# Two layers of a hybrid diffusion trunk: the second layer's modulation as elementwise products, the first step of the delta rule's inverse without matmuls, and another place for a buffer

## The chip, the cores and the metric

The kernel runs on one core of one Trainium2 chip. The metric is device time in microseconds of one execution. PE is the tensor engine, DVE the vector engine, ACT the scalar engine, POOL GpSimd, SP the sync engine, whose queue issues DMAs as POOL's does.

## What is computed

The program is one inference step of a trunk of two layers (DEPTH = 2) over 512 latent tokens and 128 context tokens, with 1024 channels. Each layer has a mixer (three parallel branches) and a feed-forward. What the change touches, cut from the reference:

```
mod = jax.nn.silu(cond) @ P['ada_w'][l] + P['ada_b'][l]          # 1024 x 6144, for two conditions
sh1, sc1, g1, sh2, sc2, g2 = jnp.split(mod[:, None, :], 6, axis=-1)
h = _rms(x, P['norm1_w'][l]) * (1 + sc1) + sh1
...                                                              # delta rule, HGRN2, attention
m = jnp.where(strict, jnp.einsum('nbhid,nbhjd->nbhij', kb, k) * decay, 0.0)
t_inv = lax.linalg.triangular_solve(eye + m, ...)                # inverse of eye + m, unit lower triangular
u = t_inv @ (v * beta[..., None]); w = t_inv @ (kb * jnp.exp(gc)[..., None])
...
x = x + g1 * (merged @ P['w_out'][l])
h = _rms(x, P['norm2_w'][l]) * (1 + sc2) + sh2
u = _dwconv(h @ P['w_up'][l], P['conv_ffn'][l]); a, u = jnp.split(u, 2, axis=-1)
x = x + g2 * ((jax.nn.silu(a) * u) @ P['w_down'][l])
```

## The kernel before

All 640 tokens are kept as columns; 128 channels are one tile in 128 partitions. Every large product is split into a high and a low half of each factor (hh and hl, or fh and fl, for activations, whi and wlo for weights): `k_steps` (line 907) issues six products for a block of 128 channels, 128x256 and 128x384 for each of three pairs, and `mtile` (line 914) eight such blocks for one output tile. A half tile of weights (4 blocks, 256 KB) is loaded on SP's queue into one of four raw buffers (wraw, line 839), copied to whi on ACT and subtracted to wlo on DVE (`w_tick`, line 878); the next load into a raw buffer waits for its wlo.

The order of the instructions on each engine is fixed when the program is built: `drive` (line 509) goes through the main stream (the large products) and side streams (the delta rule's two, HGRN2, attention, norm, the modulation), and takes a side stream's next piece when its due time, kept by cost formulas, is not ahead of PE's clock by more than a margin. Each engine then runs its own list in order.

The modulation of a layer is computed by a stream `ada` (line 693). For each chunk of 256 columns it loads four pieces of 128x2x256 (one chunk is 1 MB), issues eight products of cT, the condition as weights (32 columns), into 32 rows each, adds the result to `arows` on DVE (or copies it on ACT), and after `group` chunks turns `arows` into columns by two small products with c_sum. The first layer's chunks run ahead of and in the first mixer. The second layer's 24 chunks run in the first layer's feed-forward (line 2062), with two sets of raw buffers, in groups of four and with loads on POOL's queue. They must be done before the last group of the feed-forward goes down (line 2103).

The delta rule (`delta`, line 1219) handles five blocks in each layer: four heads' latent tokens and the context tokens. For a block of 4 x 128 tokens it inverts a triangular matrix by doubling: XC and XTC (the inverse of each 32x32 diagonal block and its transpose) start as beta on the diagonal (line 1303), and five steps (line 1306) merge blocks of 1, 2, 4, 8 and 16. A step is 16 products of 32x32 (`ath` by one half of XC), a masked product into `phc` on DVE, 16 products of 32x32 with the half of XTC, a 32x32-wise transpose on DVE and two subtractions. Two more merges, of 32 and 64, follow.

In the feed-forward (`ffn`, line 2045) the residual x is loaded back from DRAM by eight DMAs on POOL's queue, 320 KB each (line 2048), since its memory held the mixer's tiles. Then come the output projection with the update of x (`x_update`, line 2040, on DVE), norm, and three groups of up tiles (44 in all, with the depthwise conv on DVE) and down tiles (24). `open_f` (line 2024) allocates x first and fh after wx.

Of the kernel before, what the change touches and what calls it, by code (L numbers as in the profile page):

```python
# [7 lines left out]
F32 = mybir.dt.float32  # L8
F32R = mybir.dt.float32r
# [3 lines left out]
ALU = mybir.AluOpType  # L13
# [4 lines left out]
KD = 8  # L18
# [3 lines left out]
T = TS + TP  # L22
# [38 lines left out]
def shape_constants():  # L61
    c = np.zeros((128, N_CST), np.float32)
    p = np.arange(128)
    s, t = p[:, None], p[None, :]

    def put(i, a):
        c[:, i * 128:i * 128 + a.shape[1]] = a

    put(C_I, s == t)
    put(C_ONE, np.ones((128, 128)))  # L70
    put(C_UI, s <= t)
    put(C_LI, s >= t)
    put(C_US, s < t)
    put(C_LS, s > t)
    t32 = np.arange(32)[None, :]
    put(C_CP, np.concatenate([s % 32 == t32] + [(s % 32 // (2 << i) == t32 // (2 << i)) & (s % 32 >> i != t32 >> i)
                                                for i in range(5)], 1))
    misc = np.zeros((128, 128), np.float32)
    misc[:64, 2] = 1.0
    misc[64:, 3] = 1.0  # L80
    for g in range(4):
        for j in range(16):
            misc[32 * g + j, 8 + j] = 1.0
    for j in range(4):
        for e in range(2):
            misc[32 * j + e, 24 + 2 * j + e] = 1.0
    put(C_MISC, misc)
    nf = 16
    inv = (np.float32(10000.0) ** (-np.arange(nf, dtype=np.float32) / np.float32(nf))).astype(np.float32)
    pos = np.arange(TS)  # L90
    row, col = (pos // 64).astype(np.float32), (pos % 64).astype(np.float32)
    ang = np.where((p % 64 < 32)[:, None], row[None, :], col[None, :]).astype(np.float32) * inv[p % 16][:, None]
    put(C_COS, np.cos(ang.astype(np.float32)))
    put(C_SIN, np.sin(ang.astype(np.float32)) * np.where(p % 32 < 16, -1.0, 1.0).astype(np.float32)[:, None])
    return c
# [138 lines left out]
class Trunk:  # L234
# [325 lines left out]
    def setup(self):  # L560
# [14 lines left out]
        self.c_blk, self.c_pick = C(C_MISC)[:, 2:34], C(C_MISC)[:, 24:32]  # L575
        self.c_sum = C(C_MISC)[:, 8:24]
        self.hh = self.hp.tile([128, KD, T], F32R, name="hh")
        self.hl = self.hp.tile([128, KD, T], F32R, name="hl")
# [113 lines left out]

    def ada(self, l, chunks, raws, arows, gap=0.0, group=2, start=None):


        issued = 0
        at = []
# [20 lines left out]
        for n, j in enumerate(chunks):  # L718
# [22 lines left out]
            for q, j in enumerate(chunks[n - group + 1:n + 1]):  # L741
# [7 lines left out]
                self.post(("mod", l, j))  # L749
        self.post(("ada", l, chunks[-1]))  # L750

    def ada_tiles(self, pool, sets):
# [466 lines left out]
    def delta(self, l, w, batches):  # L1219
        sc, nc = dict(self.sc), self.nc  # L1220
        for name in ("ssk", "nk", "rk", "b0", "cq", "ss"):
            sc[name] = self.sc[name][:, w]
# [7 lines left out]
        for b in batches:  # L1230
# [30 lines left out]
            b0 = sc["b0"]  # L1261
            self.mul(b0, beta, bc(ssk, 1, 2))
            yield None
            pv, pq = self.psd(), self.psd()
# [30 lines left out]
            self.mul(att.ap, pqk, ph.ap)  # L1295

            small, phc = X.ap[:, 0, 0:128], ph.ap[:, 0:128]
            x64 = X.ap[:, 1, 0:256].rearrange("p (c x) -> p c x", c=4)
            self.zero(XT.ap)
            self.zero(x64)  # L1300
            XC, XTC = (xs.ap[:, o:o + 256].rearrange("p (d n) -> p d n", d=2) for o in (0, 256))
            c32 = XC.rearrange("p d (c x) -> p d c x", c=4)
            self.mul(c32, bc(bc(self.C(C_CP)[:, 0:32], 1, 4), 1, 2), bc(b0, 3, 32))
            self.cp(XTC, XC)
            yield None
            for i in range(5):
                m = 1 << i
# [516 lines left out]
    def mixer(self, l, x):  # L1824
# [13 lines left out]
        for name, shape in (("ab", [2, 2, 5, 4]), ("beta", [2, 5, 4]), ("g", [2, 5, 4]), ("gl", [2, 5, 4]), ("t0", [2, 5, 4]), ("t1", [2, 5, 4]),  # L1838
                            ("t2", [2, 5, 4]), ("ex", [3, 2, 5, 4]), ("neg", [2, 5, 4]), ("ssk", [2, 4]), ("nk", [2, 4]), ("rk", [2, 4]),
                            ("b0", [2, 2, 4]), ("cq", [2, 4]), ("ss", [2, 3, 4]), ("ssb", [3, 4]), ("ck", [3, 10]),  # L1840
                            ("s8", [3, 5, 8]),
# [171 lines left out]
        if l == 0:  # L2013
            self.spawn("ada", self.ada(0, range(8, 24), *self.ada_tiles(op, 1), 10000.0, 4))
        yield from gate_out(self.oa, "ga", self.col["norm_a"] + l)
# [8 lines left out]
    def open_f(self, l, first=False):  # L2024
        self.x_pool = ExitStack()
        fp = self.fp = self.x_pool.enter_context(self.tc.tile_pool(name=f"ffn{l}", bufs=1))
        x = fp.tile([128, KD, T], F32, name="x")
        self.N = [fp.tile([128, T], F32, name=f"N{j}") for j in range(3)]
# [5 lines left out]
        for S in self.S2[2:]:  # L2034
            self.zero_pads(S)
        self.fh = fp.tile([128, 8, T], F32R, name="fh")
        self.fl = fp.tile([128, 8, T], F32R, name="fl")
# [7 lines left out]
    def ffn(self, l, x):  # L2045
# [15 lines left out]
        if l + 1 < L:  # L2061
            self.spawn("ada", self.ada(l + 1, range(24), *self.ada_tiles(self.fp, 2), 12000.0, 4))
        n = 0
# [88 lines left out]
    def program(self):  # L2152
# [11 lines left out]
        self.spawn("ada", self.ada(0, (4, 0, 5, 1, 6, 2, 7, 3), *self.ada_tiles(init, 6), start=self.w_first))  # L2164
        self.step(self.sides[-1])
# [73 lines left out]
```

## Time and profile before

| | |
|---|---|
| time, median of 3 runs | 2730.98 us (2727.82 to 2731.32) |
| the profiled execution: its time, its span | 2731.32 us, 2729.5 us |
| PE busy | 2683.1 us (98%) |
| DVE busy | 1684.0 us (62%) |
| ACT busy | 1135.0 us (42%) |
| POOL busy | 216.1 us (8%) |
| DMA | 243.62 MB, 89 GB/s in the mean |
| large products of the mixers and feed-forwards | line 320, `mm` |
| small products of the side streams | lines 320 and 325, `sd` |

A product of two f32 tiles is two instructions on PE, so a group of eight shows as x16. The engine's name PEld stands for the loading of the stationary operand. The program's stages by time: the start to some 45 us, the first mixer to some 840, the first feed-forward to some 1385, the second mixer to some 2195, the second feed-forward to the end.

### The profile page before, as it was taken

What the parts mean: (1) busy time and instruction counts of PE and PEld (TensorE: products, weight loads), DVE (VectorE), ACT (ScalarE), POOL (GpSimd) and SP (SyncE); (2) the same over time, 40 slices, a digit from 0 to 9 for tenths busy, and PEclk for the clock granted to TensorE, in tenths of its full rate; (3) what the DMA queues carried; (4) which work ended last, traced back from release to release, by engine and by line L of the source; (5) the groups of instructions that cost most, each with busy time, mean ns of one, the idle gap of its engine ahead of it and who ended that gap; (6) DMA issues with size and microseconds to landing.
All of it is one profiled execution on the core that took longest, in us unless ns stands there. A gap on an engine that the chain in (4) does not pass through costs nothing.

```text
span 2729.5 us, 60705 instructions
## 1 busy us (share of the span) xinstructions
PE 2683.1 (98%) x25046; PEld 2558.5 (94%) x25046; DVE 1684.0 (62%) x4039; ACT 1135.0 (42%) x2619; POOL 216.1 (8%) x352
## 2 busy tenths in 40 slices
PE   8999999999999999999999999999999999999999
PEld 6999989989999999999999889899999999999999
DVE  6787865656545763554667887667566357545464
ACT  5555455534323431322345455545444244323232
POOL 1100101221001021120001001000000000000000
PEclk9999999999999999999999999999999999999999
DMA  8212223534225144443233112122222341222222
GB/s 265 71 39 53 67 57 96 158 114 126 59 76 161 58 144 132 147 143 101 80 92 83 47 45 67 49 74 73 57 61 55 82 124 56 78 73 75 77 76 80
DMA packets 356036, 243.62 MB, mean 89 GB/s; under 512 B 18069, under 2 KB 339137, under 8 KB 355632
## 3 DMA queue, kind: packets, MB, share of 16 engines
q1 hardware_dynamic: 334896, 175.94, 23.2%
q0 software_dynamic: 20432, 63.28, 7.1%
q8 instruction: 197, 3.23, 0.5%
q14 instruction: 79, 0.65, 0.1%
q10 hardware_dynamic: 432, 0.52, 0.1%
HBM read 225.79 MB, written 13.89 MB: 88 GB/s over the span
## 4 chain that ended last, share of the span: by engine, by line
PE 89%; DVE 6%; ACT 2%; issue 1%; DMA 1%; SPq 0%; ACTq 0%; DVEq 0%
PE mm L320 73%; PE sd L320 13%; PE sd L325 2%; DVE sl L355 1%; ACT sl L345 1%; DVE ex L355 1%; DMA wraw<-in_w_up_dram 1%; ACT ex L345 1%; DMA ar<-in_ada_w_dram 1%; DVE wlo L355 0%; SPq L430 0%; DVE N L368 0%; DVE Cv L368 0%; DVE x L368 0%; DVE ex L368 0%
## 5 line engine op out<-in xcount | busy, mean ns | idle before, releaser
L320 PE MATMUL mm<-hh,whi 128*128 128x256 f32 (+2 forms) x3696 | 873.8, 320 | 7.0 <-DVE x L368 6.0
L320 PE MATMUL mm<-hl,whi 128*128 128x256 f32 (+2 forms) x3696 | 841.6, 311 | 1.2 <-DVE hl L368 1.2
L320 PE MATMUL mm<-hh,wlo 128*128 128x256 f32 (+1 forms) x3632 | 835.8, 309 | 0.0
L320 PEld LDWEIGHTS mm<-hh,whi 128*128 128x128 f32 (+1 forms) x3696 | 644.3, 187 | 36.3 <-issue 25.1
L320 PEld LDWEIGHTS mm<-hl,whi 128*128 128x128 f32 (+1 forms) x3696 | 664.8, 187 | 4.0 <-DVE hl L368 1.8
L320 PEld LDWEIGHTS mm<-hh,wlo 128*128 128x128 f32 x3632 | 662.8, 188 | 0.0
L355 DVE TENSOR_TENSOR wlo<-wraw,whi 128x512 fp32r<-128x512 f32 x598 | 402.8, 680 | 369.6 <-ACT whi L345 368.6
L345 ACT ACTIVATE whi<-wraw 128x512 fp32r<-128x512 f32 x602 | 368.0, 618 | 282.4 <-PE mm L320 243.2
L368 DVE SCALAR_TENSOR_TENSOR Cv<-S,V,Cv 128x642 f32<-128x642 f32 x240 | 210.3, 883 | 2.2
L345 ACT ACTIVATE sl<-sd 128x512 f32<-128x512 f32 (+5 forms) x232 | 97.1, 429 | 195.3 <-PE sd L320 109.5
L345 ACT ACTIVATE sl<-sl 128x512 f32<-128x512 f32 (+6 forms) x224 | 119.4, 543 | 137.9 <-DVE sl L355 91.3
L320 PE MATMUL mm<-fh,whi 128*128 128x256 f32 (+1 forms) x704 | 166.7, 311 | 0.0
L320 PE MATMUL mm<-fl,whi 128*128 128x256 f32 (+1 forms) x704 | 164.7, 308 | 0.0
L320 PE MATMUL mm<-fh,wlo 128*128 128x256 f32 (+1 forms) x704 | 164.7, 308 | 0.0
L320 PE MATMUL sd<-sl,sl 128*32 128x32 f32 (+4 forms) x3384 | 156.8, 229 | 5.1 <-DVE sl L355 4.2
L430 POOL DMA_DIRECT2D ar<-in_ada_w_dram x160 | 113.3, 712 | 535.1 <-PE sd L320 528.5
L355 DVE TENSOR_TENSOR sl<-sl,sl 128x512 f32<-128x512 f32 (+2 forms) x212 | 148.9, 740 | 10.6 <-ACT sl L345 9.4
L320 PEld LDWEIGHTS sd<-sl,sl 128*32 128x32 f32 (+3 forms) x3384 | 124.8, 128 | 29.5 <-issue 12.6
L345 ACT ACTIVATE S<-mm 128x512 f32<-128x512 f32 x204 | 77.9, 435 | 160.9 <-PE mm L320 160.8
L368 DVE SCALAR_TENSOR_TENSOR x<-mm,mod,x 128x256 f32<-128x256 f32 (+1 forms) x192 | 74.6, 434 | 105.0 <-PE mm L320 100.6
L373 DVE TENSOR_SCALAR Cv<-S,V 128x642 f32<-128x642 f32 x104 | 57.7, 558 | 124.1 <-ACT S L345 123.9
L320 PEld LDWEIGHTS mm<-fh,whi 128*128 128x128 f32 x704 | 127.5, 188 | 3.3 <-issue 3.3
(264 smaller groups left out, 3250.9 us busy)
## 6 DMA issues: line engine op xcount, KB each, us to landing
wraw<-in_w_in_dram SPq DMA_DIRECT2D x264, 256.0 KB, 3.0
wraw<-in_w_up_dram SPq DMA_DIRECT2D x176, 256.0 KB, 2.9
ar<-in_ada_w_dram POOLq DMA_DIRECT2D x160, 256.0 KB, 4.1
wraw<-in_w_down_dram SPq DMA_DIRECT2D x64, 256.0 KB, 2.8
wraw<-in_w_branch_dram SPq DMA_DIRECT2D x48, 256.0 KB, 2.8
ar<-in_ada_w_dram SPq DMA_DIRECT2D x32, 256.0 KB, 6.1
wraw<-in_w_out_dram SPq DMA_DIRECT2D x32, 256.0 KB, 3.1
wraw<-in_w_down_dram SPq DMA_DIRECT2D x32, 192.0 KB, 2.5
```

Source lines behind the costliest of these rows:

```text
L320: self.nc.tensor.matmul(out, lhsT, rhs, start=start, stop=stop)
L325: self.nc.tensor.transpose(out, in_, self.c_i[:k, :k])
L345: self.nc.scalar.activation(out=out, in_=in_, func=func, scale=scale, bias=bias, **kw)
L355: self.nc.vector.tensor_tensor(out, a, b, op=op)
L368: self.nc.vector.scalar_tensor_tensor(out=out, in0=a, scalar=s, in1=b, op0=op0, op1=op1)
L373: self.nc.vector.tensor_scalar(out, a, s1, None, op0=op0)
L430: (self.nc.gpsimd if queue == "pool" else self.nc.sync).dma_start(out=out, in_=in_)
```

## The change

**The second layer's modulation** is no longer `ada` but a new stream `ada_rest`: 12 chunks of 512 columns, each in eight steps. A step loads one piece of 128x512 on SP's queue into one of four buffers, and DVE multiplies it by the condition's column of cT (one number in each partition) and adds it to an accumulator, once for each of the two conditions. After two chunks four products with a block of ones sum the 128 partitions into 32 rows each, ACT copies the result, and four small products turn it into columns.

**The delta rule's first step** (blocks of two) is done without products on PE: each row's neighbour is fetched by a shuffle within 32 partitions (`bs`), and the entry next to the diagonal is a product of numbers. XTC is formed first and XC is its transpose. Steps 2 to 5 are as before.

**fh** is allocated ahead of x in the feed-forward's pool, so x lies where wx and N began before.

```diff
-    def ada(self, l, chunks, raws, arows, gap=0.0, group=2, start=None):
+    def ada(self, l, chunks, raws, arows, group, start=None, gap=0.0):
...
+    def ada_rest(self, l, chunks, pool, gap):
+        raws = [pool.tile([128, 512], F32, name=f"ar{i}") for i in range(4)]
+        accs = [pool.tile([128, 2, 512], F32, name=f"acc{i}") for i in range(2)]
+        ar = accs[1][:, 0]
+        steps = [(j, k) for j in chunks for k in range(KD)]
+        at = []
+
+        def issue():
+            if len(at) < len(steps):
+                j, k = steps[len(at)]
+                at.append(self.dma(raws[len(at) % 4], self.i["ada_w"][l, k * 128:(k + 1) * 128, j * 512:(j + 1) * 512], "sync"))
+
+        issue()
+        issue()
+        for n, (j, k) in enumerate(steps):
+            self.cur.now = max(at[n], self.clk["pe"] + gap)
+            yield None
+            issue()
+            raw, acc, q = raws[n % 4], accs[n // KD % 2], n // KD % 2
+            for e in range(2):
+                c = self.cT[:, k, 6 + e:7 + e]
+                if k:
+                    self.stt(acc[:, e], raw, c, acc[:, e], ALU.mult, ALU.add)
+                else:
+                    self.ts(acc[:, e], raw, c, ALU.mult)
+            if k < KD - 1 or not q:
+                continue
+            yield None
+            ps = self.psd()
+            for g in range(4):
+                self.mm(ps[32 * g:32 * g + 32], self.c_one[:, 0:32], accs[g // 2][:, g % 2])
+            self.cp(ar, ps)
+            yield None
+            ps = self.psd()
+            for b in range(4):
+                self.mm(ps[:, 4 * b:4 * b + 4], ar[:, b * 128:(b + 1) * 128], self.c_pick[:, 0:8:2])
...
@@ delta @@
+            bs = sc["bs"]
+            self.shuffle(bs, b0, [i ^ 1 for i in range(32)])
+            for d in range(2):
+                self.stt(bs[:, d], bs[:, d], self.c_par[:, d:d + 1], b0[:, d], ALU.mult, ALU.mult)
...
-            self.mul(c32, bc(bc(self.C(C_CP)[:, 0:32], 1, 4), 1, 2), bc(b0, 3, 32))
-            self.cp(XTC, XC)
+            c32, t32 = (a.rearrange("p d (c x) -> p d c x", c=4) for a in (XC, XTC))
+            self.mul(t32, bc(bc(self.C(C_CP)[:, 0:32], 1, 4), 1, 2), bc(b0, 3, 32))
+            for g in range(4):
+                r = slice(32 * g, 32 * g + 32)
+                self.mul(phc[r].rearrange("p (c x) -> p c x", c=4), ath.c4[r, :, r], bc(self.C(C_CP)[r, 32:64], 1, 4))
+            self.mul(c32, bc(phc.rearrange("p (c x) -> p c x", c=4), 1, 2), bc(bs, 3, 32))
+            self.sub(XTC, XTC, XC)
+            self.vtr(xs.ap[:, 0:256], xs.ap[:, 256:512])
             yield None
-            for i in range(5):
+            for i in range(1, 5):
...
@@ open_f @@
+        if not first:
+            self.fh = fp.tile([128, 8, T], F32R, name="fh")
         x = fp.tile([128, KD, T], F32, name="x")
...
-        self.fh = fp.tile([128, 8, T], F32R, name="fh")
...
@@ ffn @@
-            self.spawn("ada", self.ada(l + 1, range(24), *self.ada_tiles(self.fp, 2), 12000.0, 4))
+            self.spawn("ada", self.ada_rest(l + 1, range(12), self.fp, 3000.0))
```

The built order shows the change at three places. First POOL's queue at the start of the first feed-forward, where x comes back from xspill; the pieces named ar after it belong to the second layer, those ahead of it to the first. Before:

```order
L430 DMA ar_3_5919<-in_ada_w_dram 128x2x256
L430 DMA x<-xspill 128x640 x8
L430 DMA ar_0_10865<-in_ada_w_dram 128x2x256
L430 DMA ar_1_10866<-in_ada_w_dram 128x2x256
L430 DMA ar_2_10867<-in_ada_w_dram 128x2x256
```

Of the change, POOL's queue at the same place, and under it SP's queue from the last weights of the output projection on:

```order
L432 DMA ar_3_5785<-in_ada_w_dram 128x2x256
L432 DMA x<-xspill 128x640 x8
L432 DMA xspill<-x 128x640 x5
L894 MEMSET wraw 128x4x16 x2
L432 DMA xspill<-x 128x640
```

```order
L432 DMA wraw<-in_w_out_dram 128x4x128 x7
L432 DMA wraw<-in_w_up_dram 128x4x128 x6
L432 DMA ar_10740<-in_ada_w_dram 128x512
L432 DMA ar_10741<-in_ada_w_dram 128x512
L432 DMA wraw<-in_w_up_dram 128x4x128 x2
L432 DMA ar_10742<-in_ada_w_dram 128x512
L432 DMA wraw<-in_w_up_dram 128x4x128
L432 DMA ar_10743<-in_ada_w_dram 128x512
```

On POOL nothing follows the reload until x is written out at the layer's end; the second layer's pieces stand on SP, behind six weights of the up tiles, and from there on one by one between them.

Second, DVE's list in the first feed-forward's up tiles (Cv are the conv's outputs, fl the low half of its result, arows the old sums, acc the new accumulators). Before:

```order
L355 TENSOR_TENSOR arows_10874<-arows_10874,sd_74 128x256
L355 TENSOR_TENSOR wlo<-wraw,whi 128x512
L368 SCALAR_TENSOR_TENSOR Cv_82<-S_80,V,Cv_82 128x642
L355 TENSOR_TENSOR Cv_82<-Cv_81,Cv_82 128x642
L355 TENSOR_TENSOR fl<-Cv_82,fh 128x512
```

Of the change:

```order
L370 SCALAR_TENSOR_TENSOR acc_10744<-ar_10743,cT,acc_10744 128x512 x2
L357 TENSOR_TENSOR wlo<-wraw,whi 128x512
L357 TENSOR_TENSOR fl<-Cv_82,fh 128x512
L370 SCALAR_TENSOR_TENSOR Cv_83<-S_9899,V,Cv_83 128x642
L357 TENSOR_TENSOR fl<-Cv_82,fh 128x128
L375 TENSOR_SCALAR acc_10745<-ar_10740,cT 128x512 x2
```

A pair of products on an accumulator now stands ahead of nearly each wlo. In PE's list six groups stand in place of 24 chunks; each begins right behind the last pair of its second chunk.

Third, DVE's list in a block of the delta rule (ex_683 and ex_684 hold XC and XTC, ex_691 and ex_692 phc, sd the results of PE). Before:

```order
L355 TENSOR_TENSOR ex_683<-cst,sc_b_667 128x256
L355 TENSOR_TENSOR wlo<-wraw,whi 128x512
L355 TENSOR_TENSOR ex_691<-sd_72,cst 128x128
L368 SCALAR_TENSOR_TENSOR Cv_84<-Cv_83,V,Cv_84 128x642
L384 STREAM_TRANSPOSE ex_1239<-sd_73 128x128
L355 TENSOR_TENSOR ex_683<-ex_683,sd_73 128x64x2
L355 TENSOR_TENSOR ex_683<-ex_683,ex_1239 128x64x2
```

Of the change:

```order
L357 TENSOR_TENSOR ex_684<-cst,sc_b_667 128x256
L357 TENSOR_TENSOR ex_692<-ex_692,cst 32x128 x4
L357 TENSOR_TENSOR ex_684<-ex_692,sc_bs 128x256
L357 TENSOR_TENSOR ex_684<-ex_684 128x256
L386 STREAM_TRANSPOSE ex_684<-ex_684 128x256
L357 TENSOR_TENSOR wlo<-wraw,whi 128x512 x2
L357 TENSOR_TENSOR ex_692<-sd_72,cst 128x128
```

The two instructions that read sd in the first step are gone, and DVE goes from the diagonal to blocks of two without PE.

## Rows read from the trace of the kernel before

**Rows 1.** Page, part 1: busy time, share of the span, instructions, whole run.

```profile
PE 2683.1 (98%) x25046; PEld 2558.5 (94%) x25046; DVE 1684.0 (62%) x4039; ACT 1135.0 (42%) x2619; POOL 216.1 (8%) x352
```

**Rows 2.** Busy by stage: stretch, us, busy us (instructions) per engine, clock, DMA, GB/s.

```profile
940.00:1280.00 340.00, 340.00 (x2514) 321.35 (x2512) 176.06 (x318) 97.40 (x199) 62.39 (x88) 1.00 0.45 137
...
1600.00:1800.00 200.00, 193.44 (x3071) 180.12 (x3059) 146.55 (x416) 101.89 (x268) 16.76 (x30) 0.98 0.21 57
```

**Rows 3.** PE timeline round one chunk's modulation products: start, us, engine, line, op.

```profile
954.33 0.46 PE L320 MATMUL mm<-hl,whi 128*128 128x256 f32 x2
954.63 0.45 PE L320 MATMUL mm<-hh,wlo 128*128 128x256 f32 x2
955.01 1.07 PE L320 MATMUL sd<-ar,cT 128*32 128x256 f32 x16
...
956.41 0.46 PE L320 MATMUL mm<-hl,whi 128*128 128x256 f32 x2
```

**Rows 4.** PE timeline, the four small products that close a group of chunks.

```profile
985.80 0.51 PE L320 MATMUL sd<-cst,arows 128*128 128x8 f32 x4
```

**Rows 5.** Busy in 29-us stretches of the first feed-forward, columns as in rows 2.

```profile
940.00:969.00 29.00, 29.00 (x215) 27.44 (x214) 19.55 (x30) 10.22 (x22) 5.66 (x8) 1.00 0.45 137
...
998.00:1027.00 29.00, 29.00 (x215) 27.45 (x214) 16.88 (x26) 9.78 (x21) 5.66 (x8) 1.00 0.46 141
```

**Rows 6.** DVE timeline, two instructions back to back in the first feed-forward.

```profile
945.66 0.88 DVE L368 SCALAR_TENSOR_TENSOR Cv<-S,V,Cv 128x642 f32<-128x642 f32 x1
946.46 0.68 DVE L355 TENSOR_TENSOR fl<-Cv,fh 128x512 fp32r<-128x512 f32 x1
```

**Rows 7.** DVE groups by form, whole run: the one nearest to the new product.

```profile
L368 DVE SCALAR_TENSOR_TENSOR Cv<-sl,V,Cv 128x512 f32<-128x512 f32 x16 | 11.9, 745 | 0.0
```

**Rows 8.** PE's waits, whole run: who waited for whom, us, times, longest.

```profile
PE sd L320 <- DVE sl L355: 4.8, 8, 1.8
```

**Rows 9.** POOL timeline, reload of x in the first feed-forward.

```profile
839.58 4.27 POOL L430 DMA_DIRECT2D x<-xspill  x8 [159.42 <-PE mm L320]
...
849.62 3.52 POOL L430 DMA_DIRECT2D ar<-in_ada_w_dram  x5 [1.65 <-issue]
```

**Rows 10.** Chain of waits there: start, us, what was waited for.

```profile
842.69 16.83 DMA wraw<-in_w_up_dram
```

**Rows 11.** PE timeline there, the first product after the wait.

```profile
863.00 0.87 PE L320 MATMUL mm<-hh,whi 128*128 128x256 f32 x2 [5.97 <-DVE x L368]
```

**Rows 12.** Busy in 2-us stretches behind it, columns as in rows 2.

```profile
864.00:866.00 2.00, 2.00 (x9) 2.00 (x9) 2.00 (x5) 1.49 (x3) 0.00 (x0) 0.50 0.05 15
```

**Rows 13.** POOL timeline, reload of x in the second feed-forward.

```profile
2196.72 4.25 POOL L430 DMA_DIRECT2D x<-xspill  x8 [329.44 <-PE mm L320]
```

**Rows 14.** Busy just behind that reload, columns as in rows 2.

```profile
2205.00:2210.00 5.00, 5.00 (x36) 5.00 (x35) 0.12 (x2) 0.63 (x1) 0.00 (x0) 1.00 1.07 349
```

**Rows 15.** PE timeline round the two small stages of one delta-rule step.

```profile
325.15 0.46 PE L320 MATMUL mm<-hh,wlo 128*128 128x256 f32 x2
325.54 0.53 PE L320 MATMUL sd<-ex,ex 32*32 32x32 f32 x32
325.88 0.48 PE L320 MATMUL sd<-sl,ex 32*32 32x32 f32 x32
...
326.69 0.46 PE L320 MATMUL mm<-hl,whi 128*128 128x256 f32 x2
```

**Rows 16.** DVE groups by form, whole run: products of the delta rule.

```profile
L355 DVE TENSOR_TENSOR ex<-sd,cst 128x128 f32<-128x128 f32 x50 | 14.1, 285 | 8.3 <-PE sd L320 8.2
...
L355 DVE TENSOR_TENSOR ex<-cst,sc_b 128x256 f32<-128x256 f32 x6 | 2.5, 416 | 0.0
```

**Rows 17.** DVE timeline, eight instructions on 32 partitions in the delta rule.

```profile
348.16 2.12 DVE L379 COPY ex<-ex 32x256 f32<-32x256 f32 x8
```

**Rows 18.** PE timeline late in the second mixer.

```profile
1756.05 1.08 PE L325 MATMUL sd<-cst,ex 128*128 128x128 f32 x4 [3.42 <-DVE ex L355]
```

**Rows 19.** Page, part 6: DMA issues on SP's queue, KB each, us to landing.

```profile
ar<-in_ada_w_dram SPq DMA_DIRECT2D x32, 256.0 KB, 6.1
```

More of the change, by code (lines that the diff above doesn't have):

```diff
@@ L80, in shape_constants @@
     misc[64:, 3] = 1.0
+    misc[:, 40] = p % 2 == 0
+    misc[:, 41] = p % 2 == 1
     for g in range(4):
@@ L576, in setup @@
         self.c_sum = C(C_MISC)[:, 8:24]
+        self.c_par = C(C_MISC)[:, 40:42]
         self.hh = self.hp.tile([128, KD, T], F32R, name="hh")
@@ L750, in ada @@
         self.post(("ada", l, chunks[-1]))
+    def ada_rest(self, l, chunks, pool, gap):
[32 more added lines that the diff above has]
+                self.mm(ps[:, 4 * b:4 * b + 4], ar[:, b * 128:(b + 1) * 128], self.c_pick[:, 0:8:2])
+            cols = ps[:, 0:16].rearrange("p (b q c) -> p q b c", b=4, q=2)
+            for i, m in enumerate((j - 1, j)):
+                d = slice(4 * m, 4 * m + 4)
+                c0 = self.col["ada_b"] + l * 48 + 4 * m
+                self.add(self.mod[l][:, d, :], cols[:, i], bc(self.V[:, c0:c0 + 4], 2, 2))
+                for first, a, w_ in ((2, self.a1, "norm1"), (8, self.a2, "norm2")):
+                    if first <= m < first + 2:
+                        k0 = 4 * (m - first)
+                        c1 = self.col[w_] + l * 8 + k0
+                        self.stt(a[l][:, k0:k0 + 4, :], self.mod[l][:, d, :], 1.0, bc(self.V[:, c1:c1 + 4], 2, 2), ALU.add, ALU.mult)
+        self.post(("ada", l, 23))
     def ada_tiles(self, pool, sets):
@@ L1220, in delta @@
         sc, nc = dict(self.sc), self.nc
-        for name in ("ssk", "nk", "rk", "b0", "cq", "ss"):
+        for name in ("ssk", "nk", "rk", "b0", "bs", "cq", "ss"):
             sc[name] = self.sc[name][:, w]
@@ L1301, in delta @@
             XC, XTC = (xs.ap[:, o:o + 256].rearrange("p (d n) -> p d n", d=2) for o in (0, 256))
-            c32 = XC.rearrange("p d (c x) -> p d c x", c=4)
-            self.mul(c32, bc(bc(self.C(C_CP)[:, 0:32], 1, 4), 1, 2), bc(b0, 3, 32))
-            self.cp(XTC, XC)
+            c32, t32 = (a.rearrange("p d (c x) -> p d c x", c=4) for a in (XC, XTC))
[6 more added lines that the diff above has]
+            self.vtr(xs.ap[:, 0:256], xs.ap[:, 256:512])
             yield None
-            for i in range(5):
+            for i in range(1, 5):
                 m = 1 << i
@@ L1839, in mixer @@
                             ("t2", [2, 5, 4]), ("ex", [3, 2, 5, 4]), ("neg", [2, 5, 4]), ("ssk", [2, 4]), ("nk", [2, 4]), ("rk", [2, 4]),
-                            ("b0", [2, 2, 4]), ("cq", [2, 4]), ("ss", [2, 3, 4]), ("ssb", [3, 4]), ("ck", [3, 10]),
+                            ("b0", [2, 2, 4]), ("bs", [2, 2, 4]), ("cq", [2, 4]), ("ss", [2, 3, 4]), ("ssb", [3, 4]), ("ck", [3, 10]),
                             ("s8", [3, 5, 8]),
@@ L2013, in mixer @@
         if l == 0:
-            self.spawn("ada", self.ada(0, range(8, 24), *self.ada_tiles(op, 1), 10000.0, 4))
+            self.spawn("ada", self.ada(0, range(8, 24), *self.ada_tiles(op, 1), 4, gap=10000.0))
         yield from gate_out(self.oa, "ga", self.col["norm_a"] + l)
@@ L2163, in program @@
             self.dma(xin[t], self.i["x_sample"][0, t * 128:(t + 1) * 128, :] if t < 4 else self.i["x_prompt"][0], "sync")
-        self.spawn("ada", self.ada(0, (4, 0, 5, 1, 6, 2, 7, 3), *self.ada_tiles(init, 6), start=self.w_first))
+        self.spawn("ada", self.ada(0, (4, 0, 5, 1, 6, 2, 7, 3), *self.ada_tiles(init, 6), 2, self.w_first))
         self.step(self.sides[-1])
```

## The prediction

> **What bounds the kernel now.** I read the page first. The tensor engine is busy for 2683.1 of 2729.5 us [rows 1], so only work taken off it, or one of its few waits, shortens the run. Then busy time by stage: in the first feed-forward PE is busy for 340.00 of 340 us and DVE for 176.06, late in the second mixer PE for 193.44 and DVE for 146.55 of 200 [rows 2]. PE sets the pace in both, and in the mixer DVE is the next engine. Then PE's timeline at the places that the change touches, the chain of waits where PE stands still, and the pace of DVE in the stretch that gets new work. The sum is made against the profiled execution, 2731.3 us, 0.3 above the median of the three runs.
>
> **Part 1, the second layer's modulation: PE.** In the first feed-forward 24 chunks each put 16 small products between the large ones. Two large products start 0.30 us apart; round a chunk the starts at 954.63 and 956.41 are 1.78 apart with two such spacings inside, so a chunk costs 1.78 - 0.60 = 1.18 us [rows 3], and 24 cost 28.3. Six times a group is closed by four small products, 0.51 us [rows 4], 3.1 in all. Removed: 31.4 us of PE, in a stretch where PE never waits, so it all counts. Added, six times: four products of 512 columns into 32 rows, as many columns in all as one old chunk (4 x 512 against 8 x 256), so I take 1.18; and eight-column sums twice as many as before, 2 x 0.51. That is 6 x 2.2 = 13.2 us. No row shows the 512-column form in 32 rows. The bounds are 0.6 us (as it has half the instructions) and 2.4 (if the four did not run side by side as well as the eight do); I take the row with the same number of columns. Net: -18.2 us, between -21.8 and -10.9.
>
> **Part 1: DVE.** DVE gets 192 products of 128x512, two in a step, 96 steps; the new order has a step about every 25 large products, 3.6 us, so 8 steps, or 16 of these DVE products, in 29 us. DVE is busy for 16.88 to 19.55 us of 29 between a group's first and last up tiles [rows 5], mean 18.2. Nearest row for a new product: three operands in SBUF, 745 ns [rows 7]. Instructions start before the one ahead has ended: the row with 0.88 us is followed after 0.80 [rows 6]. So a new product takes 0.665 of DVE's time, 16 take 10.6, and the two additions of 256 columns that go give back half a product each, some 0.7: 28.1 of 29 us. DVE is then full to 97% in the up tiles, with much room in the down tiles. The staging of weights (wlo, on DVE) runs up to three half tiles ahead of its use, some 10 us, which covers a lag of a few us. Not covered are the six sums: the order puts each right behind the last product of its chunk pair, so PE waits for DVE's lag. Nearest row: where a product waits for a DVE result, 4.8 us in 8 waits, 0.6 each [rows 8]. Six cost 3.6 us. The bounds are 0 and rival B.
>
> Here a rule speaks against the change. The Trainium skill, "VectorE: DVE Perf Modes", section "The DRAIN you can't avoid", says that the next Vector instruction does not start until the pipeline of the one before is empty, and that chaining does not avoid it; it grants further on that an instruction that is not held starts earlier. By the first sentence durations would add without overlap, which is rival B; the starts above are 0.08 us closer than that.
>
> The loads move from POOL's queue to SP's: 96 of 256 KB, between the weights' own. POOL's issuing held nobody. On SP each load stands behind a weight load that waits for a wlo; it is issued two steps, 7.2 us, ahead of use. I take no cost; rival E says when there is one.
>
> **Part 2, the reload of x.** Before, POOL issues the eight loads of x and at once eight loads for the modulation, the last five at 849.62 [rows 9]. The chain of waits then stands for 16.83 us on one weight load [rows 10], and PE waits 5.97 us until 863.00 [rows 11]. Behind that the granted clock is 0.50, the 1.2 GHz level, after an idle of 6 us [rows 12], and from 863.0 to about 866 that costs 1.5 us. The second feed-forward has the same reload and no modulation loads behind it [rows 13], and there PE is busy for 5.00 of 5 us while the DMA engines are full [rows 14]. After the change SP issues the first of the new loads after the first up tiles, far behind. So the wait and the slow clock go: -7.5 us. What is late next is x itself, whose loads start when they did; the chain names a weight there and not x. The other bound is 0, if the weights alone are late (rival C).
>
> **Part 3, the moved buffer.** x moves up by the size of fh. In the built order the reload still waits for the same last branch product, and at the layer's end the tiles of the next mixer take fh's place where they took x's. I cost it at nothing: what hides it is that the reload's start is set by PE.
>
> **Part 4, the delta rule.** Ten blocks (five in each layer) lose one of five steps. A step is two stages of 32 small products: large products at 325.15 and 326.69 are 1.54 apart with two spacings inside, so a step costs 1.54 - 0.60 = 0.94 us [rows 15], ten cost 9.4. On DVE a step's four instructions of some 285 ns go, 1.1 us; added are four products on 32 partitions (0.265 each, as eight take 2.12 [rows 17]), three instructions of 128x256 at 416 ns [rows 16] and three tiny ones, some 0.5: 2.8 us. Net +1.7 us on DVE in each block, 17 in all, less a copy on ACT. DVE is at 73% in the mixer [rows 2] and the block also loses two round trips between PE and DVE, so I take 0, with bounds -8 and +17. The lower one is from a wait of 3.42 us on DVE in the tail of a block [rows 18], followed by a slow clock as in part 2, and the like: such waits may go with a shorter chain.
>
> **Sum.** 2731.3 - 18.2 + 3.6 - 7.5 - 9.4 = 2699.8; against the median 2699.5.
>
> **The rivals.**
> A, the sum above, 0.55. F, the mixers' waits on DVE go as well: 2691, chance 0.05.
> B, DVE becomes the bound in the up tiles: durations add. The 18.2 us hold some 28 instructions, each 0.08 us longer, 20.4; 16 times 0.745 more and 0.7 less make 31.6 us in 29, 9% too much. Some 35 up tiles of 7 us carry steps, 245 us, so PE loses 22 us in place of 3.6: 2718. For it: only 3% of room by my own count. Against: the overlap in rows 6, and room in the down tiles. 0.15.
> C, the reload's wait stays, because x and the weights alone fill the DMA engines: 2707. Against it stands the second layer [rows 14]. 0.12.
> D, the delta rule's extra DVE work is exposed, each block holding PE by 1.7 us: 2717. 0.08.
> E, slower: the new loads arrive late. A step's product waits in DVE's queue for its load, that load stands on SP behind a weight load, and that one waits for a wlo behind the same step. The one row for such loads on SP, at the start of the run, shows 6.1 us to landing [rows 19] against 7.2 us of lead. Of each step's delay 0.1 us is covered by DVE's room; the rest holds PE in some 68 steps of the up tiles. From 0.6 us a step (0.5 x 68 = 34) the gain of 32 is gone; at 1 us, 2699.5 - 3.6 + 61 = 2757. Against: in that stage the DMA engines are busy for 0.45 of the time only [rows 2]. 0.05.
>
> **The numbers.** Less than 0.2% (5.5 us) can't be told from no change. A, B, C, D and F are all faster by more, 0.95 in all, of which 0.02 goes to no change, for two bad ends at once: 0.93; same 0.02; slower 0.05. The range takes in F and the lower bounds, and B and D: 2687 to 2719. That leaves out E and the sum of several bad ends.
>
> **What will show it.** In the new profile: the first feed-forward free of the 16-product groups, with six groups of 512 columns of about 1.2 us; DVE near 27 to 28 us busy in 29 in its up tiles, and PE still at 29.00 but for waits of under 1 us at the six sums; no gap in PE after the first reload of x and a clock of 1.00 there; four steps in a delta block instead of five. PE gaps spread over the up tiles that end on wlo would show B, gaps of DVE that end on the new loads E, a gap near 857 C. The prediction is wrong if PE's busy share in the first feed-forward falls below 0.95.

## The result, and the profile after

The changed kernel takes 2695.24 us, median of four runs (2692.89 to 2695.62), against 2731.15 (2727.82 to 2732.93) before: ratio 0.9869, 95% interval 0.9854 to 0.9884, that is 35.9 us or 1.3% less. The forecast was 2699.5. The execution in the profile took 2692.89 us with a span of 2690.8.

Page, part 1, of the changed kernel, the line that answers to [rows 1]:

```profile
PE 2653.5 (99%) x24094; PEld 2539.1 (94%) x24094; DVE 1805.9 (67%) x4267; ACT 1132.8 (42%) x2609; POOL 148.5 (6%) x256
```

PE's busy time fell by 29.6 us, and span less busy time, its idle time, from 46.4 to 37.3 us. To see where, the run is cut at three marks that both traces have: the first reload of x begins on POOL, the first xspill of the first feed-forward's end, the second reload. Busy time by stage before (columns as in rows 2):

```profile
0.00:839.60 839.60, 819.08 (x8966) 757.55 (x8967) 548.30 (x1490) 397.18 (x960) 94.41 (x159) 1.00 0.34 98
839.60:1362.60 523.00, 515.75 (x3695) 495.59 (x3694) 285.46 (x534) 166.32 (x346) 72.31 (x104) 0.99 0.40 122
1362.60:2196.70 834.10, 820.82 (x8795) 780.85 (x8794) 559.57 (x1494) 397.31 (x958) 45.08 (x82) 1.00 0.24 66
2196.70:2729.50 532.80, 527.41 (x3597) 524.52 (x3595) 290.70 (x523) 174.19 (x358) 4.25 (x8) 1.00 0.27 80
```

The same four stages of the changed kernel:

```profile
0.00:833.20 833.20, 815.60 (x8646) 754.25 (x8647) 555.45 (x1525) 395.97 (x955) 94.52 (x159) 1.00 0.34 98
833.20:1335.00 501.80, 499.12 (x3383) 487.94 (x3382) 392.60 (x692) 166.97 (x346) 4.26 (x8) 1.00 0.41 127
1335.00:2158.00 823.00, 812.09 (x8475) 773.33 (x8474) 567.25 (x1529) 395.67 (x953) 45.50 (x83) 1.00 0.24 67
2158.00:2690.80 532.80, 526.66 (x3597) 523.55 (x3595) 290.62 (x523) 174.21 (x358) 4.25 (x8) 1.00 0.28 80
```

The first mixer is 6.4 us shorter, the first feed-forward 21.2, the second mixer 11.1, the second feed-forward not at all. These make 38.7 us, as the profiled execution is the fastest of its four; a second profile of the changed kernel (after_again, below) has 4.8, 21.1, 10.3 and -0.4. In the feed-forward 16.6 of the 21.2 us are PE's busy time and 4.6 its idle time; DVE is busy for 107 us more there and POOL for 68 us less. So the feed-forward came out close to the forecast for the modulation with the reload (22.1), and the mixers gave 17.5 us, 15.1 in the second profile, in place of 9.4.

The up tiles, 29-us stretches that answer to [rows 5], and one with a sum in it:

```profile
940.00:969.00 29.00, 29.00 (x199) 29.00 (x198) 28.85 (x46) 10.71 (x23) 0.00 (x0) 1.00 0.49 151
998.00:1027.00 29.00, 29.00 (x199) 29.00 (x198) 26.75 (x45) 8.56 (x17) 0.00 (x0) 1.00 0.51 163
...
1150.00:1179.00 29.00, 27.98 (x183) 25.52 (x182) 22.91 (x39) 9.32 (x20) 0.00 (x0) 1.00 0.33 103
```

DVE is full in the first of them and PE still busy for 29.00; PE loses time only where a sum stands. DVE's timeline there, the rows that answer to [rows 6] and [rows 7]:

```profile
954.78 1.41 DVE L370 SCALAR_TENSOR_TENSOR acc<-ar,cT,acc 128x512 f32<-128x512 f32 x2
956.11 0.68 DVE L357 TENSOR_TENSOR wlo<-wraw,whi 128x512 fp32r<-128x512 f32 x1
```

Two products start 1.33 us ahead of the next instruction: 0.665 each, though one lasts 745 ns. PE's timeline round the first sum and the picking products behind it, as [rows 3] and [rows 4]:

```profile
973.12 0.46 PE L322 MATMUL mm<-hh,wlo 128*128 128x256 f32 x2
973.51 1.53 PE L322 MATMUL sd<-acc,cst 128*32 128x512 f32 x8
974.97 0.56 PE L322 MATMUL mm<-hh,whi 128*128 128x256 f32 x2
975.37 0.46 PE L322 MATMUL mm<-hl,whi 128*128 128x256 f32 x2
975.67 0.45 PE L322 MATMUL mm<-hh,wlo 128*128 128x256 f32 x2
975.96 0.95 PE L322 MATMUL sd<-cst,acc 128*128 128x4 f32 x8
976.77 0.54 PE L322 MATMUL mm<-hh,whi 128*128 128x256 f32 x2
977.15 0.46 PE L322 MATMUL mm<-hl,whi 128*128 128x256 f32 x2
```

By the forecast's way of counting the sum costs 975.37 - 973.12 - 0.60 = 1.65 us with its wait, the picking (the four small products that turn the sums into columns) 977.15 - 975.67 - 0.60 = 0.88. Counted so, the six sums cost 1.65, 1.19, 1.84, 3.90, 1.29 and 3.23 us, 13.1 in all. The waits for accumulators are split: those of weight loads (PEld) on acc, and of products (PE); here of 915 to 1300 us:

```profile
PE sd L322 <- DVE acc L370: 1.4, 2, 1.0
...
PEld sd L322 <- DVE acc L370: 5.1, 6, 1.9
```

At the first reload of x, POOL's timeline has nothing behind the eight loads; [rows 9] had eight more. And PE's busy time at the place of [rows 11], some 17 to 23 us after the reload began:

```profile
833.18 4.28 POOL L432 DMA_DIRECT2D x<-xspill  x8 [159.32 <-PE mm L322]
```
```profile
850.00:855.00 5.00, 5.00 (x37) 5.00 (x36) 3.95 (x8) 3.03 (x6) 0.00 (x0) 1.00 0.50 142
855.00:860.00 5.00, 5.00 (x37) 5.00 (x36) 3.83 (x9) 1.99 (x4) 0.00 (x0) 1.00 0.60 173
```

The wait of 5.97 us is gone, and the granted clock stays at 1.00. (A wait of 1.1 us on x follows at 891.08; the kernel before has one of that length too, besides the 5.97.)

### The profile page after: what moved, and what is told of

Read it like the earlier page. It is cut to its first block, busy times and chain, and to the rows that moved or that the text cites. A ratio compares the mean times of both kernels' runs of the same rounds, so it can differ in the third digit from the quotient of the medians.

```text
span 2690.8 us, 58963 instructions
## 1 busy us (share of the span) xinstructions
PE 2653.5 (99%) x24094; PEld 2539.1 (94%) x24094; DVE 1805.9 (67%) x4267; ACT 1132.8 (42%) x2609; POOL 148.5 (6%) x256
## 4 chain that ended last, share of the span: by engine, by line
PE 88%; DVE 8%; ACT 2%; issue 2%; DMA 1%; SPq 0%; ACTq 0%; DVEq 0%
PE mm L322 73%; PE sd L322 12%; PE sd L327 2%; DVE sl L357 1%; DVE acc L370 1%; DVE Cv L370 1%; DVE ex L357 1%; DVE wlo L357 1%; ACT sl L347 1%; DMA ar<-in_ada_w_dram 1%; DMA wraw<-in_w_up_dram 0%; DVE N L370 0%; SPq L432 0%; ACT ex L347 0%; ACT whi L347 0%
## 5 line engine op out<-in xcount | busy, mean ns | idle before, releaser
L347 ACT ACTIVATE sl<-sl 128x512 f32<-128x512 f32 (+5 forms) x220 | 117.7, 545 | 144.2 <-DVE sl L357 101.9
L357 DVE TENSOR_TENSOR sl<-sl,sl 128x512 f32<-128x512 f32 (+2 forms) x212 | 148.9, 739 | 12.1 <-ACT sl L347 9.4
L322 PEld LDWEIGHTS mm<-fl,whi 128*128 128x128 f32 x704 | 128.0, 188 | 0.0
L322 PEld LDWEIGHTS mm<-fh,wlo 128*128 128x128 f32 x704 | 127.8, 188 | 0.1
```

What stands on the lines that cost most here:

```text
L322: self.nc.tensor.matmul(out, lhsT, rhs, start=start, stop=stop)
L347: self.nc.scalar.activation(out=out, in_=in_, func=func, scale=scale, bias=bias, **kw)
L357: self.nc.vector.tensor_tensor(out, a, b, op=op)
```

## The experiments

The kernel before, measured beside them, took 2731.2 to 2732.0 in the median. "Of before" means ratios to it. Differences to the changed kernel are to its 2695.24 us; measured once more beside the last experiment it took 2695.55.

**Three parts of the change, each alone, and the loads' queue alone.** e1_modulation takes the new function and its two calls, e2_delta the delta rule's lines, e3_fh the two lines of fh. e4_sp is the kernel before with one line changed in ada:

```diff
-                                 "pool" if gap else "sync")
+                                 "pool" if gap and l == 0 else "sync")
```

> The second layer's modulation alone as changed (its products on the vector engine, its loads on SP); delta rule and buffer as before. My theory: 18.2 us off TensorE in the first feed-forward, 3.6 back at the six sums, and 7.5 us off at the reload of x: 22.1 us faster than the kernel before, some 2709. Rival B (DVE bound in the up tiles): 4 us faster or less, with TensorE's gaps spread over the up tiles. Rival C (the reload's wait stays): 14.6 us faster. Rival that the larger gain measured lies in this part: about 29 us faster, with the mixers' part at 9.

2711.04 us, 0.9929 of before (0.9914 to 0.9945): 20.2 us, with an interval of 15.0 to 23.5. That holds the 22.1 of the theory and leaves out B's 4, C's 14.6 and 29.

> The delta rule alone as changed; modulation and buffer as before. My theory: ten blocks at 0.94 us, 9.4 us faster, some 2721.5. Rival D (the extra DVE work is exposed): up to 8 us slower than before. Rival F (waits on DVE in the mixers go with the shorter chain): 15 to 17 us faster, and then most of it in the second mixer, where the wait of 3.42 us in the tail of a block and the slow clock behind it should be gone.

2713.82 us, 0.9935 (0.9922 to 0.9949): 17.4 us (13.9 to 21.3), rival F's figure and not my 9.4. Its page, part 1, and its stages by the same marks:

```profile
PE 2672.7 (99%) x24406; PEld 2549.7 (94%) x24406; DVE 1699.4 (63%) x4109; ACT 1132.0 (42%) x2609; POOL 216.5 (8%) x352
```
```profile
0.00:834.50 834.50, 816.85 (x8645) 755.54 (x8646) 555.55 (x1525) 395.72 (x955) 94.38 (x158) 1.00 0.34 98
834.50:1355.10 520.60, 515.16 (x3696) 495.01 (x3695) 285.67 (x534) 166.79 (x346) 72.36 (x105) 1.00 0.41 123
1355.10:2180.00 824.90, 813.29 (x8474) 774.71 (x8473) 567.39 (x1529) 395.27 (x953) 45.47 (x82) 1.00 0.24 66
```

PE's busy time falls by 10.4 us and its idle time by 6.3, from 46.4 to 40.1. Of the 16.7 us of span 5.1 come in the first mixer, 2.4 in the feed-forward (the reload's wait there is 4.16 in place of 5.97) and 9.2 in the second mixer. There the 3.42 us wait of [rows 18] is gone; the longest on the same tile is 0.7. Before, the granted clock fell with that wait, by ten-us stretches:

```profile
1750.00:1760.00 10.00, 6.58 (x40) 6.42 (x39) 3.78 (x17) 5.06 (x15) 1.63 (x3) 0.74 0.25 73
1760.00:1770.00 10.00, 10.00 (x128) 9.63 (x127) 7.06 (x15) 4.63 (x9) 0.27 (x1) 0.92 0.11 28
```

By one-us stretches the clock is 0.50 from 1755, still in the wait, to 1761 and 0.65 in the next us; PE is busy at it from 1756 on, which loses 2.8 us. In e2_delta one stretch of 20 us at 1680 still has 0.91 (some 1.8 us lost), in the changed kernel no stretch from 1380 to 1880 is below 1.00. Waits and slow clock move about between kernels: in the first mixer the changed kernel has 0.92 and 0.91 at 330 to 350, where before had 1.00, and its second profile has a slow stretch at 1662 again.

Busy time holds the slow clock, so it is not yet the work saved. If busy time in each us is weighted by the granted clock, an estimate, PE's work in the two mixers falls by 12.1 us in e2_delta, and by 11.0 and 10.7 in the changed kernel's two profiles: 1.1 to 1.2 us for each of the ten steps. Its idle time there falls by 4.5, 5.3 and 4.8.

> The moved buffer alone: fh is allocated ahead of x, all else as before. My theory: no difference, within 2 us. Rival: where x lies decides when the reload of x can start; then the wait at the first reload (5.97 us, and 1.5 us of slow clock) shrinks or goes without the modulation's loads being moved, up to 7.5 us faster.

2730.42 us, 0.9998 (0.9989 to 1.0006), eleven runs: no difference. The wait at the reload is 6.0 us as before.

> The second layer's modulation stays on TensorE as before and with all its products; only its loads are issued from SP in place of POOL. My theory (these loads collide with the reload of x): if SP issues them behind the same place the collision may stay, since the first sets are asked for at the same point of the program; what SP holds ahead of them decides. If they now fall behind the weights that TensorE waits for, the wait at the reload goes, 7.5 us faster. Rival C (x and the weights alone fill the DMA engines): no difference. A third outcome: loads on SP hold up the weights behind them, slower by some us.

2724.55 us, 0.9974 (0.9964 to 0.9984): 6.7 us faster with every product left as it was. There is no wait of PE at the reload, as in the changed kernel. SP's timeline says why; the first loads of the modulation come 81 us after the reload began, at 840.71, behind weight loads that wait for free tiles:

```profile
915.63 5.50 SPq L430 DMA_DIRECT2D wraw<-in_w_up_dram  x2
921.49 3.95 SPq L430 DMA_DIRECT2D ar<-in_ada_w_dram  x8
```

The three parts alone make 20.2 + 17.4 + 0.8 = 38.4 us, together 35.9; the delta rule alone also shortens the reload's wait, which the other part removes, and that, 2.4 us, is counted twice in the first sum.

**The loads back on POOL in the changed kernel**, one word of the dma call in ada_rest:

```diff
-                at.append(self.dma(raws[len(at) % 4], self.i["ada_w"][l, k * 128:(k + 1) * 128, j * 512:(j + 1) * 512], "sync"))
+                at.append(self.dma(raws[len(at) % 4], self.i["ada_w"][l, k * 128:(k + 1) * 128, j * 512:(j + 1) * 512], "pool"))
```

> The changed kernel with its modulation loads issued from POOL in place of SP; all else as changed. My theory: what counted at the reload of x was how many loads stood right behind it on POOL; here it would be two of 256 KB in place of eight, so at most a small part of the 7.5 us comes back: 0 to 2 us slower than the changed kernel. Rival: the queue itself does it (POOL's transfers go ahead of the weights on SP): 5 to 7.5 us slower. A third: SP's extra issues cost something in the up tiles, then this one is faster.

2700.90 us, 0.9891 (0.9876 to 0.9906): 5.7 us above the changed kernel, where I had expected 0 to 2. My count was wrong: four loads went out within 5 us, not two, as there are four raw tiles. POOL's timeline, the chain of waits there, PE's wait and the busy time:

```profile
834.73 4.28 POOL L432 DMA_DIRECT2D x<-xspill  x8 [159.32 <-PE mm L322]
839.06 0.54 POOL L432 DMA_DIRECT2D ar<-in_ada_w_dram  x1
...
843.85 0.54 POOL L432 DMA_DIRECT2D ar<-in_ada_w_dram  x1 [0.77 <-DMA x<-xspill]
```
```profile
836.85 15.39 DMA wraw<-in_w_up_dram
```
```profile
855.73 0.87 PE L322 MATMUL mm<-hh,whi 128*128 128x256 f32 x2 [3.55 <-DVE x L370]
```
```profile
850.00:855.00 5.00, 2.18 (x15) 1.91 (x13) 1.59 (x4) 1.05 (x2) 0.00 (x0) 1.00 0.58 149
855.00:860.00 5.00, 4.27 (x19) 4.30 (x20) 3.99 (x8) 2.99 (x6) 0.00 (x0) 0.66 0.42 116
```

A weight load again takes 15.39 us ([rows 10] had 16.83), PE idles 3.55 us, and the clock is slow behind it. In the changed kernel the load at this place is issued at 835.30 and its tile read at 846.66, 11.4 us later with x alone beside it, and PE doesn't wait. So some 11 us are covered, and four loads of 256 KB behind x bring most of the stall back. The Trainium skill, "DMA: Bandwidth & Descriptors", section "Queues, rings and completion order", says that each DMA engine takes in turn the queues that it has work for. That would explain the delay, as a queue filled early then takes turns from the weights' queue, but no run here isolates the turns; the runs show that the queue, with what is issued into it early, decides.

**The delta rule without its first step.** In e2_delta the lines that took the place of the step are left out, those that make bs too, and the old start stands:

```diff
-            c32, t32 = (a.rearrange("p d (c x) -> p d c x", c=4) for a in (XC, XTC))
-            self.mul(t32, bc(bc(self.C(C_CP)[:, 0:32], 1, 4), 1, 2), bc(b0, 3, 32))
...
-            self.mul(c32, bc(phc.rearrange("p (c x) -> p c x", c=4), 1, 2), bc(bs, 3, 32))
-            self.sub(XTC, XTC, XC)
-            self.vtr(xs.ap[:, 0:256], xs.ap[:, 256:512])
+            c32 = XC.rearrange("p d (c x) -> p d c x", c=4)
+            self.mul(c32, bc(bc(self.C(C_CP)[:, 0:32], 1, 4), 1, 2), bc(b0, 3, 32))
+            self.cp(XTC, XC)
```

> The kernel with the delta rule alone changed, with the first step left out altogether: neither the products on TensorE nor those on the vector engine that took their place are there (the inverse is computed without its first step, so the outputs differ); what is left is the shorter chain. My theory: the extra DVE work is hidden, so this takes the time of the delta rule's change alone, some 2714, within 4 us. Rival D: it is exposed, each of ten blocks by up to 1.7 us and a little more for the small products: 10 to 20 us faster than that.

2712.64 us, 0.9933 (0.9919 to 0.9948), 1.2 us below e2_delta, which the spread of the runs doesn't tell from nothing. Page, part 1:

```profile
PE 2671.1 (99%) x24406; PEld 2549.5 (94%) x24406; DVE 1672.7 (62%) x3999; ACT 1133.8 (42%) x2619; POOL 216.0 (8%) x352
```

26.7 us less on DVE, 2.7 in each block where the sum had 2.8, buy 1.2 us, if anything. Rival D is out: the extra work is hidden, and the gain of e2_delta is that of the missing step.

**The pace of the steps.** e5_pace halves the gap (in ns) that the order asks for between two steps of the changed kernel:

```diff
-            self.spawn("ada", self.ada_rest(l + 1, range(12), self.fp, 3000.0))
+            self.spawn("ada", self.ada_rest(l + 1, range(12), self.fp, 1500.0))
```

> The changed kernel with the pace of the modulation's steps halved from 3000 to 1500 in its order, so that the same 192 products of the vector engine stand closer together. My theory: as the order stands DVE has some 3% of room in the up tiles; closer steps ask for more than DVE has, the lag grows beyond what staging covers, and TensorE waits in the up tiles: 10 to 50 us slower than the changed kernel, with TensorE's waits ending on wlo or on the sums of acc. Rival: the order's own reckoning of DVE spreads the steps anyway, or the lag is absorbed; within 5 us of the changed kernel.

2702.53 us, 0.9894 (0.9880 to 0.9909), 7.3 us above the changed kernel: between my 10 to 50 and the rival's 5. The steps came every 2.7 us in place of 3.8. Two stretches of its up tiles, and the waits of PE and of weight loads on acc, 915 to 1300 us:

```profile
947.00:976.00 29.00, 27.39 (x179) 24.92 (x178) 28.84 (x48) 10.45 (x22) 0.00 (x0) 1.00 0.49 158
976.00:1005.00 29.00, 28.00 (x183) 25.53 (x183) 28.97 (x46) 9.70 (x19) 0.00 (x0) 1.00 0.54 173
```
```profile
PE sd L322 <- DVE acc L370: 3.9, 4, 1.6
...
PEld sd L322 <- DVE acc L370: 10.0, 9, 2.5
```

DVE is full for longer, and PE pays at the sums: 13.9 us of waits on acc in place of 6.5. This is not rival B as forecast, as none of PE's waits there ends on wlo. DVE itself waits 4.8 us in six places for the pieces of 128x512 (in the changed kernel nowhere), so part of the lag is late loads; the two were not told apart.

**The sums deferred.** In e9_defer there are three accumulators in place of two, and each sum comes behind the first step of the next pair:

```diff
-            if k < KD - 1 or not q:
-                continue
-            yield None
-            ps = self.psd()
...
+            if late is not None:
+                yield from close(late)
+                late = None
+            if k == KD - 1 and n // KD % 2:
+                late = n
```

> The changed kernel with each of the six sums put behind the first step of the next chunk pair (a third pair of accumulators, so that the next products need not wait), instead of right behind the last product it reads. My theory: the 3.6 us that I put down for the six sums are waits for DVE's lag; with a step between, they go: 3 to 5 us faster than the changed kernel. Rival: the waits are the price of the sum's form itself and of the steps around it, no difference (within 1.5 us).

2689.93 us (2689.04 to 2692.78), 0.9847 of before (0.9832 to 0.9861). This is 5.3 us below the changed kernel, whose four runs all lie above these four; the intervals of the two ratios overlap at their ends. The list of PE's waits from 915 to 1300 us has no line for acc any more, that of weight loads one of 0.4 us, on ACT's copy. The feed-forward from the reload to the first xspill is 496.5 us, 5.3 less than the changed kernel's 501.8. The first sum:

```profile
974.97 0.46 PE L322 MATMUL mm<-hh,wlo 128*128 128x256 f32 x2
975.35 1.07 PE L322 MATMUL sd<-acc,cst 128*32 128x512 f32 x8
976.35 0.56 PE L322 MATMUL mm<-hh,whi 128*128 128x256 f32 x2
976.74 0.46 PE L322 MATMUL mm<-hl,whi 128*128 128x256 f32 x2
```

Without a wait it costs 976.74 - 974.97 - 0.60 = 1.17 us. DVE is as full as before in the first up tiles (28.94 and 28.85 of 29), with PE at 29.00.

**The deferred sums at a slower pace**, 4000 in place of 3000, and the changed kernel once more beside it:

> The kernel with the deferred sums, its steps at a pace of 4000 in place of 3000, so that DVE is less full in the up tiles. My theory: with the sums deferred DVE at 28.9 of 29 us in the first two stretches costs TensorE nothing any more, so nothing is gained: within 2 us of the kernel with the deferred sums, some 2690. Rival: DVE's fullness still holds TensorE a little at each tile: 3 us or more faster, with TensorE's busy time nearer to 29 of 29. A third: the later end pushes the last sums against the end of the feed-forward, slower.

> The changed kernel once more, beside the other one on the same chip, as the base for it: 2695, as measured first, within 2 us by every theory. If the deferred sums are worth something, the kernel with them stays 3 to 5 us below this.

after_again: 2695.55 us, 0.9871 (0.9855 to 0.9888), as at first. e12_slow: 2708.75 us, 0.9921 (0.9906 to 0.9936), 19 us above e9_defer: not my theory but the third outcome. PE's timeline at the last sum, and the clock behind it:

```profile
1332.90 2.58 PE L322 MATMUL sd<-acc,cst 128*32 128x512 f32 x4 [14.17 <-DVE acc L370]
```
```profile
1320.00:1330.00 10.00, 0.00 (x0) 0.00 (x0) 9.23 (x16) 0.83 (x2) 0.00 (x0) 0.66 0.47 137
1330.00:1340.00 10.00, 6.41 (x20) 4.20 (x21) 4.82 (x10) 1.53 (x3) 0.00 (x0) 0.50 0.04 16
```

The end of the feed-forward waits in program order for the modulation's last chunk (`self.wait(("ada", l + 1, 23))`), so the steps that are left are put out in a row and PE stands for 14.17 us, then runs at half clock. Before that, PE is busy for 29.00 of every 29 us from 918 to 1295 (e9_defer: 339.85 of 340 from 940 to 1280): the emptier DVE gained nothing.

**The first layer's late chunks too**, in the changed kernel:

```diff
-            self.spawn("ada", self.ada(0, range(8, 24), *self.ada_tiles(op, 1), 4, gap=10000.0))
+            self.spawn("ada", self.ada_rest(0, range(4, 12), op, 5000.0))
```

> The changed kernel with the first layer's late chunks of modulation (chunks 8 to 23, beside the merge of the first mixer) done by products on the vector engine as well. My theory: 16 chunks at 1.18 and four closing groups at 0.51 go from TensorE, 20.9 us; four sums of 2.5 us are added, with their waits: 10 to 12 us faster than the changed kernel, some 2684. Rival: DVE or its lag holds TensorE in the merge and eats it: no gain, or slower.

2709.23 us, 0.9923 (0.9906 to 0.9939), 14 us above the changed kernel, where I had expected 10 to 12 below. PE's timeline and a stretch of busy time:

```profile
733.28 2.00 PE L322 MATMUL sd<-sl,sl 128*64 128x128 f32 x16 [2.90 <-DVE sl L381]
739.39 1.87 PE L322 MATMUL sd<-cst,acc 128*128 128x4 f32 x8 [3.11 <-ACT acc L347]
751.16 1.97 PE L327 MATMUL sd<-cst,sl 128*128 128x128 f32 x8 [4.34 <-DVE sl L375]
```
```profile
740.00:780.00 40.00, 30.93 (x182) 27.31 (x183) 22.53 (x57) 11.03 (x27) 0.00 (x0) 0.76 0.19 52
```

The first and the third wait are for attention's chain (maximum, exponent, scaling on DVE and ACT), the second is for ACT's copy of the modulation's own sum. From 730.4 to 764.3 us no large product stands in PE's timeline to run beside them; in the changed kernel PE is busy for 40.00 of the 40 us from 740.

> As e7_both (the first layer's late chunks by products on the vector engine too), with steps at a pace of 3000 in place of 5000, so that they end earlier, before the attention's last tiles. My theory: in e7_both the loss came from the late end (the attention's tiles ran after the large products with nothing beside them, TensorE waited 3 to 4 us at each and its clock fell to 0.76 from 740 to 780); ending earlier keeps that cover: 5 to 12 us faster than the changed kernel. Rival: it is the vector engine's load, which the closer pace makes worse: as slow as e7_both or slower, 10 to 25 us above the changed kernel.

2717.70 us, 0.9949 (0.9933 to 0.9966), 22 us above the changed kernel. My theory of the late end fell, the rival's 10 to 25 us hold; the same stretch is worse:

```profile
740.00:780.00 40.00, 27.48 (x142) 20.72 (x143) 18.36 (x56) 11.05 (x29) 0.00 (x0) 0.64 0.08 24
```

DVE is fuller in the stretches ahead of it (35.51 and 36.34 of 40 us from 460 to 540; in e7_both 33.69 and 35.68, in the changed kernel 24.43 and 28.25), and attention's products stand alone some 8 to 10 us later than in e7_both. That the backlog of DVE is the whole cause was not isolated.

The fastest kernel here is e9_defer: the change, with deferred sums.

## Why the prediction was right, and the term that was too small

The sign and the size held, 2695.2 against 2699.5, inside the range. The total came nearer than its largest error, as the errors had both signs. By its steps:

- **PE in the modulation, -18.2 net.** Right: e1_modulation gains 13.5 us more than e4_sp, against 18.2 - 3.6 = 14.6. The price taken for a sum, 1.18 between 0.6 and 2.4, is 1.17 without a wait (e9_defer); the row with the same number of columns was the right one to take. The picking came to 0.88 at the first sum, against 1.02. (The lower bound adds up to -21.7, not -21.8.)
- **DVE, 28.1 of 29 us.** Right at the start of the up tiles (28.85); in later 29-us stretches of up tiles DVE is busy for 23 to 27, and for 18.6 to 24 where down tiles, which have no convolution, stand in the stretch. The 96 steps ran from 918 to 1283 us, every 3.8 in the mean against the forecast's 3.6. The overlap was read rightly from [rows 6]: 0.665 us a product. The Trainium skill, "VectorE: DVE Perf Modes", section "The DRAIN you can't avoid", says that the next instruction starts only when the pipeline is empty, and that one that is not held starts earlier. The rows of this change agree with the second: products of 745 ns start 0.665 us apart; whether any was held no run here shows. Rival B did not happen at this pace, and at the closer pace of e5_pace PE's waits were still those at the sums.
- **Six waits, +3.6.** The place was right and the size low: the six sums cost 13.1 us where six at 1.17 would cost 7.0, so 6.1 of waits; 5.3 us come back when the sums are deferred.
- **The reload, -7.5.** Right, with its cause: 6.7 us with the queue alone (e4_sp), and 5.7 lost again with the queue back (e6_pool). Rival C is out. The slow clock was read too short: it is 0.50 not until 866 but until 867, and 0.80 in the next us, 2.2 us lost in place of 1.5. With 5.97 that is the 8.1 us by which this stage is shorter in e4_sp's profile.
- **fh, 0.** Right: -0.8 us, interval on both sides of no change.
- **SP's queue, 0 (rival E).** Right: the loads of the modulation on SP land in 3.3 us in the median (6.1 in [rows 19], where there were only those at the start), and no group of PE's waits ends on them in the up tiles.
- **The delta rule, -9.4.** This is the term that was mis-sized. The sum took ten steps at 0.94 on PE and then, for the shorter chain between PE and DVE, "so I take 0, with bounds -8 and +17". The part measures 17.4 us alone: 9.4 and the whole of the lower bound. Some of that is not the chain: a step is worth 1.1 to 1.2 us of PE's time and not 0.94, 11 to 12 in all, and 2.4 come at the reload. What the sum put at 0 is PE's idle time in the mixers, which falls by some 5 us. (In e2_delta's profile 2.3 us more of slow clock in the mixers stand against these gains.) The argument for 0 was DVE's load of 73%, and e8_skip shows that the DVE work added costs 1.2 us, if anything. Rival F, at 2691 with a chance of 0.05, named this, and the longest of the waits, 3.42 us in [rows 18], stood in the rows.

In gains, 8.0 us too little for the delta rule (17.4 less 9.4) and 1.9 too much for the modulation (22.1 less 20.2) make 6.1. Together the parts give 35.9, 1.7 less than the 37.6 of the two alone, which leaves the 4.4 us between the gain forecast (31.5) and measured. What stays open is how the delta rule's idle time splits into single waits: they move from kernel to kernel, as the slow clock does, and between the two profiles of the changed kernel the mixers differ by 2.4 us.

## What to carry to other kernels

Here the work moved to an engine with room cost TensorE nothing while it lagged, except where TensorE asked for the result at once: put such a request behind the next piece of work, and end all of it before the program itself asks for the last one. Room has to be looked up stage by stage: products of the same kind that left TensorE busy in the up tiles made the kernel 14 to 22 us slower in the mixer, where the same engine carries a chain that TensorE waits for. When a dependent chain loses a step, count the round trips as well as the products, and when loads collide with a reload, look first at which queue issues them and how early.

## What the runs showed of the hardware that was not expected

A few loads issued early on another queue hold up a weight load: beside x alone it took some 11 us, of which TensorE felt nothing, with four loads of 256 KB behind x 15.39, with eight 16.83. So four brought back 5.7 of the 6.7 us that eight had cost (e6_pool, e4_sp).

An idle time of 3 to 4 us of PE is followed by some us at the lower clock level more than once (mean granted clock 0.66 in e6_pool, 0.74 before, here in stretches of 5 and 10 us), and 14 us of waiting by a stretch wholly at 0.50, the 1.2 GHz level. So a wait can cost more than its length: in the second mixer before, 3.42 us of waiting and 2.8 of slow clock.
